# Smaller turns for a recurrence that runs beside attention, with its matrix products a turn later

## The chip, the core and the metric

One NeuronCore of a Trainium2 chip runs the whole kernel. The metric is the device time of one execution in microseconds; lower is better. The five engines have a queue each and take it in order: TensorE (PE in the profile, with its weight loads as PEld), VectorE (DVE), ScalarE (ACT), GpSimd (POOL) and SyncE (SP), which here issues nearly all DMA transfers.

## The reference, cut to what matters

Two layers, each with three token mixers side by side on 1024 latent and 256 context tokens, then an output projection, a gated residual and a squared-ReLU MLP. The mixers are a Fourier group, a bidirectional mLSTM recurrence (4 heads of 96, called the recurrence below) and multi-head latent attention (4 heads):

```
h = modulate(rmsnorm(x, g_norm1[l]), sh1, sc1)
pf, mq, mk, mv, mo, mg, cq, ckv, kr = split_proj(h @ w_in[l])
y_f = fourier_mix(pf)
hf, _ = mlstm_direction(fwd, st_f, False)      # state C_new = decay*C + (wk*k)^T v, chunk by chunk
hb, _ = mlstm_direction(bwd, st_b, True)       # out h = (s@v + w_inter*(q@C)) / max(|den|, exp(-m_t))
y_m = mlstm_output(hf, hb, mo, g_mlstm[l])     # rmsnorm(hf + hb) per head, gated by sigmoid(mo)
y_a = merge_heads(blocked_attend(qn, qr, (lat_keys, ctx_keys)))
x = x + ga1 * (concat([y_f, y_m, y_a]) @ w_out[l])
x = x + ga2 * sqrelu_mlp(modulate(rmsnorm(x, g_norm2[l]), sh2, sc2), w_up[l], w_down[l])
```

## The kernel before, in words

Python code emits instructions, and a scheduler then puts each engine's instructions into a fixed order by priority (the place in the program, unless raised) and by when it expects their inputs; an engine's order on the chip is that order. So where code is written decides the order only in part.

Per layer the kernel runs the input projections, then the attention stage, then the output projection and the MLP. The change touches the attention stage alone. Its main loop goes over blocks (a head, and 512 latent or 256 context queries), and inside over the 10 (context: 2) tiles of 128 keys. One such tile is called a step here, numbered from 0: 88 steps in layer 0, 80 in layer 1. A step computes scores `s` (three products: L138, L143, L144), their exponentials `PT` on ScalarE (L1140), and the value product `v<-PT,Vt` (L1141), which adds to the block's sum. Layer 0 has one PSUM buffer for `s`, layer 1 has two.

TensorE's time between scores and value product is filled with other work. A list `bg` holds the preparation of later blocks: keys and queries (`K`, `Q`, products of `ckn`, `wkv`, `cqn`, `wq`), the maxima of the scores (product L1003 into `m`, maximum `mx` on VectorE L1004, transposed as a row by L1013) and the division at a block's end (`ya`, `rc`, L1031 and L1037). After each step `side_work` pulls turns from a generator: first `mlstm`, then, when that is exhausted, `fourier`. A turn is what the generator emits up to its next `yield`.

`mlstm` has two passes over chunks of 128 tokens. The first (18 steps, two directions `d`) transposes keys (`kt`, L834), weights the values (`wv`, VectorE L839), multiplies them (L842), updates the state `C` on VectorE (L850) and stores it in DRAM (`dC`). It is one turn a step. The second pass takes the chunks in token order. Its first turn is the score product `sp` (L885). Then, for each direction, one turn loads `Mb`, `Wb` and the stored state `Cp`, builds the weights `tm` (L897, ScalarE's exponentials L900, L901) and `qw` (L906), multiplies (`po`, L912 with `tm`, L914 with `qw` and `Cp`) and divides (`dn`, `hd`, L918 to L922). The function `tail` normalises the chunk before and transposes it (L868) for the store of `ym` into `dy`, in one turn. Of these 18 + 4 x 10 = 58 turns of layer 0, 23 are pulled ahead of the main loop, one for each entry of the first `bg` list, at raised priority; the rest goes out at a rate of `nm_ / (tot * RM[l])` turns a step, where `tot` is 78 steps in layer 0 and 70 in layer 1. `RM` thus is the share of the steps over which the recurrence is spread. `fourier` follows at a rate of its own, `nf_ / (tot * RF)`.

The last block (L1119 on) closes the generators' pools, opens the ring of weight buffers in their place, loads `w_out` (`wf`, split by ScalarE and GpSimd into `wr` high and low), loads the mixers' outputs from `dy` (`q`, `qf`, split by ScalarE and VectorE into `A`) and starts the output projection (`mm`, L138, L140, L141) between its steps. In all order listings below, numbers behind names count buffers; `x`, in `s<-Q,x`, is a key tile.

Of the kernel before, what the change touches and what calls it, by code (L numbers as in the profile page):

```python
# [22 lines left out]
C_ID, C_CC, C_SS, C_MK, C_AR, C_RP, C_AC = 0, 128, 256, 384, 640, 1152, 2176  # L23
NCST = 2178
BIG = 1e30
RM = (0.5, 0.8)
GR = (2, 0, 2, 2, 2, 1)
RF = 0.18
LT = (3,)
# [34 lines left out]
def build(tc, A, out, dbg=None):  # L64
# [41 lines left out]
    V, S, G, PE = nc.vector, nc.scalar, nc.gpsimd, nc.tensor  # L106
# [44 lines left out]
    hk = {}  # L151
# [276 lines left out]
    for l in range(2):  # L428
# [384 lines left out]
        def mlstm(mlp_):  # L813
# [12 lines left out]
            for p in range(9):  # L826
                for d in range(2):
                    ci = order[d][p]
                    kc = T(mlp_, [96, 4, 128], tag="kc", bufs=2)
                    nc.sync.dma_start(kc, dkh[:, :, tok(ci)])  # L830
                    vc = load_v(ci)
                    ps = T(psL, [128, 512], tag="l")
                    for h in range(4):
                        PE.transpose(ps[:, h * 96:(h + 1) * 96], kc[:, h, :], ident[:96, :96])  # L834
                    kt = T(mlp_, [128, 512], tag="tm", bufs=2)
                    S.copy(kt[:, :384], ps[:, :384])
                    wcol = wkT[:, 64 * d + ci:64 * d + ci + 31:10]
                    wv = T(mlp_, [128, 4, 128], tag="Mb", bufs=2)
                    V.tensor_tensor(wv[:, :, :97], vc, wcol.unsqueeze(2).to_broadcast([128, 4, 97]), ALU.mult)  # L839
                    pc = T(psL, [128, 512], tag="l")  # L840
                    for h in range(4):
                        PE.matmul(pc[:96, h * 97:(h + 1) * 97], kt[:, h * 96:(h + 1) * 96], wv[:, h, :97], start=True, stop=True)  # L842
                    C = T(mlp_, [96, 4, 128], tag=("qw", "Wb")[d], bufs=2)
                    pv = pc[:96, :388].rearrange("p (h e) -> p h e", h=4)
                    if p == 0:
                        S.copy(C[:, :, :97], pv)
                    else:
                        for h in range(4):
                            dcol = 40 * d + 10 * h + ci
                            V.scalar_tensor_tensor(C[:, h, :97], prev[d][:, h, :97], decb[:, dcol:dcol + 1], pv[:, h], ALU.mult, ALU.add)  # L850
                    prev[d] = C
                    nc.sync.dma_start(dC[d, ci].rearrange("p (h e) -> p h e", h=4), C[:, :, :97])
                    yield
            def tail(ci, hs, mo):
                hsum = hs[0]
                V.tensor_tensor(hsum, hs[0], hs[1], ALU.add)
                S.activation(hs[1], hsum, AF.Square)
                v4 = T(mlp_, [128, 4], tag="v4", bufs=2)
                V.tensor_reduce(v4, hs[1], AX.X, ALU.add)
                V.tensor_scalar(v4, v4, 1.0 / 96, EPS, ALU.mult, ALU.add)  # L860
                y4 = T(mlp_, [128, 4], tag="y4", bufs=2)
                rstd_small(y4, v4, 4, mlp_)
                V.tensor_tensor(hsum, hsum, y4.unsqueeze(2).to_broadcast([128, 4, 96]), ALU.mult)
                hf = hsum.rearrange("p h e -> p (h e)")
                V.scalar_tensor_tensor(mo, mo, 1.0, hf, ALU.add, ALU.mult)
                pt = T(psL, [128, 512], tag="l")
                for i in range(3):
                    PE.transpose(pt[:, i * 128:(i + 1) * 128], mo[:, i * 128:(i + 1) * 128], ident)  # L868
                ym = T(mlp_, [128, 3, 128], tag="ym", bufs=2)
                for i in range(3):  # L870
                    S.activation(ym[:, i], pt[:, i * 128:(i + 1) * 128], AF.Copy, scale=gmh[:, 3 * l + i:3 * l + i + 1])
                nc.sync.dma_start(dy[256:640].rearrange("(i p) t -> p i t", p=128)[:, :, tok(ci)], ym)

            pend = None
            for ci in range(10 if ctx_all else 8):
# [14 lines left out]
                for d in range(2):  # L890
# [12 lines left out]
                    if not first:  # L903
                        pi = order[d][order[d].index(ci) - 1]
                        qw = T(mlp_, [96, 4, 128], tag="qw", bufs=2)
                        V.tensor_tensor(qw, qc, Wb, ALU.mult)  # L906
                        Cp = T(mlp_, [96, 4, 97], tag="Cp", bufs=2)
                        nc.sync.dma_start(Cp, dC[d, pi].rearrange("p (h e) -> p h e", h=4))
                    po = T(psL, [128, 512], tag="l")
                    for h in range(4):  # L910
                        o = po[:, h * 97:(h + 1) * 97]
                        PE.matmul(o, tm[:, h], vc[:, h], start=True, stop=first)  # L912
                        if not first:
                            PE.matmul(o, qw[:, h], Cp[:, h], start=False, stop=True)  # L914
                    pv = po[:, :388].rearrange("p (h e) -> p h e", h=4)
# [7 lines left out]
                    hs.append(hd)  # L923
                    yield
                    if d == 1 and pend is not None:
                        tail(*pend)
                        yield
                pend = (ci, hs, mo)
            tail(*pend)
            yield  # L930


# [138 lines left out]


        mlq = Pools()
        gm_ = mlstm(mlq("ml", side=other))
        bg = [k_rope] + [lambda b=b: k_piece(0, b) for b in (2, 0, 1)] + prepare(0, 0) + [lambda t=t: v_piece(0, t) for t in range(5)]
        p1 = tc.cur_priority - p0
        for f_ in bg:
            with tc.high_priority(offset=p1):
                pull(gm_, 1)
                f_()  # L1080
        fq = None
        steps = [10 if qb < 2 else 2 for _, qb in blocks]
# [19 lines left out]
                        quota["g"] = None  # L1102
                        break

        nm_ = 18 + 4 * (10 if ctx_all else 8) - len(bg) + 1
        nf_ = (7 if ctx_all else 4) * 2 + 1
        quota = dict(m=0.0, f=0.0, g=None, rm=nm_ / (tot * RM[l]), rf=nf_ / (tot * RF))
        ending = None
        for bi, (h, qb) in enumerate(blocks):
# [26 lines left out]
            for i, kt in enumerate(kts):  # L1136
                ps = T(psS, [128, 512], tag="s")
                mm3(ps[:, :nq], K[:, 0, tok(kt)], K[:, 1, tok(kt)], Q[:, 0, :nq], Q[:, 1, :nq], True, True)
                PT = T(atp, [128, 512], tag="PT", bufs=5)
                S.activation(PT[:, :nq], ps[:, :nq], AF.Exp, scale=scale)  # L1140
                PE.matmul(po[:97, :nq], Vt[kt // 2][:, kt % 2, h % 2], PT[:, :nq], start=i == 0, stop=i == len(kts) - 1)  # L1141
                if h == 1 and qb == 1 and kt % 2:
                    v_piece(1, kt // 2)
                while bg and len(bg) > nbg * (len(kts) - 1 - i) / len(kts):
                    bg.pop(0)()
                if not lastb:
                    side_work()
                elif i == 0:
                    while bg:
                        bg.pop(0)()  # L1150
                    wo.append(wtile(A["w_out"][l, 0]))
                    for b in border[:-1]:
                        load_y(b)
                elif i in (1, 3, 5, 7):
                    wo.append(wtile(A["w_out"][l, len(wo)]))
                    if i in LT:
                        out_tile(LT.index(i), 0)
# [544 lines left out]
```

## Time and profile before

| | |
|---|---|
| median of 3 runs | 3015.47 us (3014.15 to 3018.77) |
| the profiled execution's own time | 3019.14 us |
| its span, first to last instruction | 3017.3 us, mean granted TensorE clock 0.962 |
| TensorE busy | 2827.9 us (94%) |
| VectorE busy | 2128.6 us (71%) |
| ScalarE busy | 1178.6 us (39%) |
| attention steps of layer 0 | about 386 to 700 us |
| attention steps of layer 1 | about 1976 to 2250 us |

Times in the profile count from the span's start. A wait in the profile is put down to the engine and the tile that came last. A row of the stretches has start and end, length, busy time of the engines with the number of instructions, the granted clock, and the DMA engines' share and rate. A row of the waits has who waited and for whom, the total in us, the number of waits and the longest. A timeline row has start, duration, engine, line, operation, and in square brackets the idle time ahead of it and what ended it.

### The profile page before, as it was taken

How to read it: one execution, taken by the hardware profiler on the slowest of the kernel's cores; microseconds unless marked ns; L12 is line 12 of the kernel's file. 1: busy time of each engine (PE TensorE's matmuls, PEld its weight loads, DVE VectorE, ACT ScalarE, POOL GpSimd, SP SyncE). 2: the span in 40 equal slices, each digit the busy share in tenths (PEclk: the TensorE clock that was granted, in tenths of full speed). 3: DMA queues.
4: the chain of work that ended last, by engine and by line, in shares of the span. 5: the costliest groups of instructions: out<-in, count | busy, mean ns of one | idle time of the engine just before them, and what ended most of it. 6: DMA issues, size and time to landing. Idle time of an engine off the chain costs nothing.

```text
span 3017.3 us, 40556 instructions
## 1 busy us (share of the span) xinstructions
PE 2827.9 (94%) x14320; PEld 2334.7 (77%) x14320; DVE 2128.6 (71%) x4170; ACT 1178.6 (39%) x2283; POOL 517.3 (17%) x517
## 2 busy tenths in 40 slices
PE   7988989989989999999999898899999999989996
PEld 6877867757878888888887787867767788868885
DVE  8769668742498898786787527468633976678887
ACT  3322245443353333243245432245433534334444
POOL 4213100011200000021125133100022000013334
PEclk7999999999999999999999999899999999999998
DMA  6514575323355544633121212455134443253321
GB/s 237 161 55 128 146 174 156 110 91 120 109 175 175 168 171 165 240 112 116 45 91 56 88 42 85 124 147 147 56 120 139 146 134 115 105 198 99 105 85 56
DMA packets 277871, 376.44 MB, mean 125 GB/s; under 512 B 63396, under 2 KB 154468, under 8 KB 276004
## 3 DMA queue, kind: packets, MB, share of 16 engines
q1 hardware_dynamic: 274788, 366.51, 39.0%
q0 software_dynamic: 576, 4.20, 0.4%
q10 hardware_dynamic: 2304, 3.15, 0.3%
q8 instruction: 113, 1.85, 0.3%
q14 instruction: 90, 0.74, 0.1%
HBM read 283.74 MB, written 90.02 MB: 124 GB/s over the span
## 4 chain that ended last, share of the span: by engine, by line
PE 59%; DVE 18%; DMA 10%; issue 6%; POOL 2%; ACT 2%; SPq 0%; DVEq 0%; POOLq 0%; ACTq 0%
PE mm L138 9%; PE mm L143 7%; PE mm L144 7%; PE v L1141 4%; PE mm L135 4%; PE mm L136 4%; PE mm L134 4%; DVE junk L235 3%; DVE A L148 2%; DVE ac L677 2%; PE mm L1466 2%; PE mm L140 2%; PE mm L141 2%; DMA wf<-in_w_mt 2%; PE t L1466 2%
## 5 line engine op out<-in xcount | busy, mean ns | idle before, releaser
L138 PE MATMUL mm<-A,wr 128*128 128x512 f32 (+1 forms) x840 | 312.9, 375 | 24.6 <-ACT rb L673 12.3
L135 PE MATMUL mm<-A 128*128 128x512 f32 (+1 forms) x654 | 251.3, 389 | 11.2 <-DVE A L148 8.9
L134 PE MATMUL mm<-A 128*128 128x512 f32 (+1 forms) x654 | 238.1, 387 | 5.6 <-ACT A L147 4.4
L136 PE MATMUL mm<-A 128*128 128x512 f32 (+1 forms) x654 | 242.9, 387 | 0.3 <-DVE A L148 0.3
L138 PEld LDWEIGHTS mm<-A,wr 128*128 128x128 f32 x840 | 161.2, 193 | 54.0 <-ACT rb L673 14.0
L143 PE MATMUL mm<-A,wr 128*128 128x512 f32 (+1 forms) x520 | 193.0, 372 | 6.2 <-DVE A L148 4.2
L144 PE MATMUL mm<-A,wr 128*128 128x512 f32 (+1 forms) x520 | 191.6, 369 | 0.0
L1141 PE MATMUL v<-PT,Vt 128*97 128x512 f32 (+1 forms) x336 | 172.8, 599 | 16.6 <-ACT PT L1140 16.1
L138 PE MATMUL mm<-A,c 128*128 128x512 f32 (+1 forms) x520 | 184.0, 355 | 4.5 <-ACT A L147 3.4
L143 PE MATMUL mm<-A,c 128*128 128x512 f32 (+1 forms) x520 | 184.3, 355 | 2.7 <-DVE A L148 2.6
L144 PE MATMUL mm<-A,c 128*128 128x512 f32 (+1 forms) x520 | 182.5, 353 | 1.3 <-DVE c L148 1.3
L148 POOL TENSOR_TENSOR wr<-wf,wr 128x512 fp32r<-128x512 f32 x88 | 123.7, 1413 | 292.1 <-ACT wr L147 230.3
L147 ACT ACTIVATE A<-wr 128x512 fp32r<-128x512 f32 x188 | 114.2, 625 | 147.9 <-PE mm L135 59.2
L147 ACT ACTIVATE A<-A 128x512 fp32r<-128x512 f32 x174 | 106.9, 625 | 160.0 <-PE mm L135 86.6
L148 DVE TENSOR_TENSOR A<-wr,A 128x512 fp32r<-128x512 f32 x146 | 128.7, 893 | 43.4 <-ACT A L147 29.0
L235 DVE SCALAR_TENSOR_TENSOR junk<-wf,t 128x512 bf16<-128x512 f32 x192 | 130.8, 681 | 33.7 <-DMA wf<-in_w_mt 32.0
L135 PEld LDWEIGHTS mm<-A 128*128 128x128 f32 x654 | 123.9, 190 | 39.4 <-DVE A L148 11.7
L1140 ACT ACTIVATE PT<-s 128x512 f32<-128x512 f32 (+1 forms) x168 | 97.0, 583 | 138.6 <-PE s L144 138.0
L134 PEld LDWEIGHTS mm<-A 128*128 128x128 f32 x654 | 123.1, 189 | 31.2 <-ACT A L147 6.8
L136 PEld LDWEIGHTS mm<-A 128*128 128x128 f32 x654 | 123.5, 189 | 25.0 <-DVE A L148 0.7
L138 PE MATMUL mm<-wr,A 128*128 128x256 f32 x464 | 133.4, 288 | 6.6 <-ACT rb L673 4.7
L143 PE MATMUL mm<-wr,A 128*128 128x256 f32 x464 | 133.1, 288 | 0.0
(497 smaller groups left out, 7802.9 us busy)
## 6 DMA issues: line engine op xcount, KB each, us to landing
wf<-in_w_mt SPq DMA_DIRECT2D x96, 256.0 KB
x<-in_w_up SPq DMA_DIRECT2D x40, 512.0 KB
r<-in_w_up SPq DMA_DIRECT2D x38, 512.0 KB
wr<-in_w_dn SPq DMA_DIRECT2D x36, 512.0 KB
gt<-in_w_mt SPq DMA_DIRECT2D x64, 256.0 KB
da<-wf SPq DMA_DIRECT2D x64, 256.0 KB
da<-p SPq DMA_DIRECT2D x64, 256.0 KB
wf<-in_w_in SPq DMA_DIRECT2D x56, 256.0 KB
```

What stands on the lines that cost most here:

```text
L134: PE.matmul(ps, lh, rh, start=first, stop=False, skip_group_check=True)
L135: PE.matmul(ps, lh, rl, start=False, stop=False, skip_group_check=True)
L136: PE.matmul(ps, ll, rh, start=False, stop=last, skip_group_check=True)
L138: PE.matmul(ps, lh, rh, start=first, stop=False)
L143: PE.matmul(ps, lh, rl, start=False, stop=False)
L144: PE.matmul(ps, ll, rh, start=False, stop=last)
L147: (hi or S).activation(dst[0], src, AF.Copy) if (hi is None or hi is S) else hi.tensor_copy(dst[0], src)
L148: (lo or G).tensor_tensor(dst[1], src, f32(dst[0]), ALU.subtract)
L235: V.scalar_tensor_tensor(junk, f, 1.0, cb[w], ALU.mult, ALU.mult, accum_out=(ga, modT[l])[kh][:, w, j:j + 1])
L1140: S.activation(PT[:, :nq], ps[:, :nq], AF.Exp, scale=scale)
L1141: PE.matmul(po[:97, :nq], Vt[kt // 2][:, kt % 2, h % 2], PT[:, :nq], start=i == 0, stop=i == len(kts) - 1)
L1466: PE.matmul(o, blk[f"B{h + 1}{q + 1}"][k][:, 128 * jj:128 * jj + 128], f[:, k, 256 * h:256 * h + 256], start=h + k == 0, stop=h * k == 3)
```

## The change

It splits the recurrence's turns. In the first pass a `yield` stands between the weighting on VectorE and the products on TensorE; in the second, between the elementwise preparation and the `po` products; in `tail`, between the normalisation and the transposes. The turns are 36 + 7 x 10 = 106 in layer 0; two instead of one are pulled for each entry ahead of the loop (46 for 23), and the count `nm_` follows. The `po` products with `tm` and the transposes in `tail` get an edge behind the latest value product: on TensorE they may not be ordered ahead of the value product that was the last one emitted. `RM` of layer 0 goes from 0.5 to 0.75; that of layer 1 stays 0.8.

```diff
-RM = (0.5, 0.8)
+RM = (0.75, 0.8)
...
                     V.tensor_tensor(wv[:, :, :97], vc, wcol.unsqueeze(2).to_broadcast([128, 4, 97]), ALU.mult)
+                    yield
                     pc = T(psL, [128, 512], tag="l")
...
+            def after_pv():
+                return behind("pv" if hk.get("pv") else None)
+
             def tail(ci, hs, mo):
...
                 V.scalar_tensor_tensor(mo, mo, 1.0, hf, ALU.add, ALU.mult)
+                yield
                 pt = T(psL, [128, 512], tag="l")
                 for i in range(3):
-                    PE.transpose(pt[:, i * 128:(i + 1) * 128], mo[:, i * 128:(i + 1) * 128], ident)
+                    with after_pv():
+                        PE.transpose(pt[:, i * 128:(i + 1) * 128], mo[:, i * 128:(i + 1) * 128], ident)
...
                         nc.sync.dma_start(Cp, dC[d, pi].rearrange("p (h e) -> p h e", h=4))
+                    yield
                     po = T(psL, [128, 512], tag="l")
                     for h in range(4):
                         o = po[:, h * 97:(h + 1) * 97]
-                        PE.matmul(o, tm[:, h], vc[:, h], start=True, stop=first)
+                        with after_pv():
+                            PE.matmul(o, tm[:, h], vc[:, h], start=True, stop=first)
...
                     if d == 1 and pend is not None:
-                        tail(*pend)
+                        yield from tail(*pend)
                         yield
...
+        hk["pv"] = None
         gm_ = mlstm(mlq("ml", side=other))
...
-                pull(gm_, 1)
+                pull(gm_, 2)
...
-        nm_ = 18 + 4 * (10 if ctx_all else 8) - len(bg) + 1
+        nm_ = 36 + 7 * (10 if ctx_all else 8) - 2 * len(bg) + 1
...
-                PE.matmul(po[:97, :nq], Vt[kt // 2][:, kt % 2, h % 2], PT[:, :nq], start=i == 0, stop=i == len(kts) - 1)
+                hk["pv"] = PE.matmul(po[:97, :nq], Vt[kt // 2][:, kt % 2, h % 2], PT[:, :nq], start=i == 0, stop=i == len(kts) - 1)
```

What it does to the order, at three places of layer 0. First TensorE at the second pass's first chunk, steps 14 and 15 before (L912 and L914 are its products; `l_4085` is the forward direction, `l_4123` the backward one):

```order
L912 MATMUL l_4085<-vc_4050,tm_4074 128x97
L914 MATMUL l_4085<-Cp_4083,qw_4081 128x97
L1141 MATMUL v_4688<-PT_4759,Vt_589_3482 97x512
L914 MATMUL l_4123<-Cp_4121,qw_4119 128x97
L912 MATMUL l_4123<-vc_4050,tm_4112 128x97
L914 MATMUL l_4123<-Cp_4121,qw_4119 128x97
L912 MATMUL l_4123<-vc_4050,tm_4112 128x97
L914 MATMUL l_4123<-Cp_4121,qw_4119 128x97
```

The same chunk now, steps 13 and 14 (L920 and L922 are L912 and L914, L1150 is L1141):

```order
L922 MATMUL l_4085<-Cp_4075,qw_4073 128x97
L920 MATMUL l_4085<-vc_4050,tm_4066 128x97
L920 MATMUL l_4123<-vc_4050,tm_4104 128x97
L922 MATMUL l_4085<-Cp_4075,qw_4073 128x97
L920 MATMUL l_4085<-vc_4050,tm_4066 128x97
L922 MATMUL l_4085<-Cp_4075,qw_4073 128x97
L1150 MATMUL v_4612<-PT_4649,Vt_588_3481 97x512
L138 MATMUL s_4679<-Q_4316,x_586_3479 128x512
L922 MATMUL l_4123<-Cp_4113,qw_4111 128x97
```

Both directions still come close together, a step earlier than before; the backward one now has a score product ahead of its products with `Cp`.

Second, TensorE at the end of the sixth block of 512, steps 63 to 65 before:

```order
L1141 MATMUL v_6356<-PT_6479,Vt_591_3484 97x512
L138 MATMUL s_6488<-Q_6099,x_586_3479 128x512
L143 MATMUL s_6488<-Q_6099,x_586_3479 128x512
L144 MATMUL s_6488<-Q_6099,x_586_3479 128x512
L1141 MATMUL v_6356<-PT_6492,Vt_592_3485 97x512
L138 MATMUL s_6501<-Q_6099,x_586_3479 128x512
L143 MATMUL s_6501<-Q_6099,x_586_3479 128x512
L144 MATMUL s_6501<-Q_6099,x_586_3479 128x512
L1141 MATMUL v_6356<-PT_6505,Vt_592_3485 97x512
```

The last of these steps now (`l<-tb,uc` and `l<-tb,uh` are Fourier products):

```order
L138 MATMUL s_6357<-Q_5805,x_586_3479 128x512
L143 MATMUL s_6357<-Q_5805,x_586_3479 128x512
L144 MATMUL s_6357<-Q_5805,x_586_3479 128x512
L138 MATMUL l_6373<-tb_6184,uc_6344 128x128
L143 MATMUL l_6373<-tb_6184,uc_6344 128x128
L144 MATMUL l_6373<-tb_6184,uc_6344 128x128
L786 MATMUL l_6373<-tb_6184,uh_6352 128x128
L787 MATMUL l_6373<-tb_6184,uh_6352 128x128
L138 MATMUL l_6379<-tb_6184,uc_6349 128x128
L143 MATMUL l_6379<-tb_6184,uc_6349 128x128
L144 MATMUL l_6379<-tb_6184,uc_6349 128x128
L1150 MATMUL v_6070<-PT_6361,Vt_592_3485 97x512
```

Steps that held nothing between scores and value product hold Fourier products.

Third, SP where the weights of the output projection are first loaded, before:

```order
L811 DMA dy_91<-yt_6091 128x1280 [waits DMAHW0_49,DVE_49,Activation_49]
L1039 DMA dy_91<-ya_6517 96x512 [waits DMAHW1_49,DVE_49]
L167 DMA wf_6760<-in_w_out 128x512 [waits DMAHW2_49,PE_49]
L167 DMA wf_6765<-in_w_out 128x512 [waits DMAHW3_49]
L167 DMA wf_6843<-in_w_out 128x512 [waits DMAHW4_49]
L1057 DMA q_1492_6771<-dy_91 128x512 [waits DMAHW5_49,DVE_49]
```

And now (L1065 is L1057, a load of the mixers' outputs; `yt` is the second and last Fourier output):

```order
L1065 DMA q_1492_6771<-dy_91 128x512 [waits DMAHW1_49,DVE_49]
L1065 DMA qf_6775<-dy_91 128x512 [waits DMAHW2_49,DVE_49]
L1065 DMA q_1494_6779<-dy_91 128x512 [waits DMAHW3_49,DMAHW1_49,DVE_49]
L1065 DMA qf_6783<-dy_91 128x512 [waits DMAHW4_49,DMAHW2_49,DVE_49]
L811 DMA dy_91<-yt_6420 128x1280 [waits DMAHW5_49,DVE_49,Activation_49]
L1065 DMA q_1496_6787<-dy_91 128x512 [waits DMAHW6_49,DMAHW3_49,DVE_49]
L167 DMA wf_6760<-in_w_out 128x512 [waits DMAHW7_49,PE_49]
L167 DMA wf_6765<-in_w_out 128x512 [waits DMAHW0_49]
L167 DMA wf_6843<-in_w_out 128x512
```

The weights' first loads have moved behind the last Fourier store and five loads of the mixers' outputs. The first product that needs them stands in step 76 of TensorE's order instead of step 72.

More of the change, by code (lines that the diff above doesn't have):

```diff
@@ L925, in mlstm @@
                     if d == 1 and pend is not None:
-                        tail(*pend)
+                        yield from tail(*pend)
                         yield
                 pend = (ci, hs, mo)
-            tail(*pend)
+            yield from tail(*pend)
             yield
```

## The prediction

> **What bounds the kernel now.** I read the page's first part, then the stretches of the two attention stages, then who waited for whom in each stretch, then the timeline at the places found.
>
> ```profile
> span 3017.3 us, 40556 instructions
> PE 2827.9 (94%) x14320; PEld 2334.7 (77%) x14320; DVE 2128.6 (71%) x4170; ACT 1178.6 (39%) x2283; POOL 517.3 (17%) x517
> ```
>
> TensorE is the bound, and the change adds and removes no matrix product. So it can only move TensorE's gaps, and what follows from gaps. The stages that it touches are these (TensorE, weight loads, VectorE, ScalarE, GpSimd busy; then granted clock and DMA):
>
> ```profile
> 427.00:456.00 29.00, 23.99 (x120) 17.41 (x119) 21.23 (x46) 11.68 (x29) 0.11 (x1) 0.88 0.58 158
> 456.00:576.00 120.00, 114.07 (x666) 86.11 (x666) 106.08 (x339) 64.40 (x165) 1.27 (x8) 1.00 0.55 154
> 576.00:629.00 53.00, 52.64 (x285) 38.89 (x284) 32.57 (x73) 21.81 (x56) 0.23 (x3) 1.00 0.10 35
> 656.00:692.00 36.00, 29.54 (x112) 20.75 (x111) 11.55 (x23) 14.34 (x27) 7.69 (x6) 0.81 0.45 135
> 1976.00:2140.00 164.00, 155.73 (x866) 119.11 (x866) 127.14 (x354) 77.11 (x179) 1.26 (x12) 0.96 0.50 126
> 2140.00:2215.00 75.00, 74.99 (x344) 52.69 (x343) 42.70 (x86) 35.09 (x70) 12.59 (x10) 0.98 0.35 113
> 443.60:450.40 6.80, 6.40 (x19) 4.32 (x18) 4.21 (x10) 2.13 (x7) 0.00 (x0) 0.50 0.63 147
> 668.90:682.60 13.70, 10.14 (x33) 7.44 (x31) 2.79 (x7) 3.23 (x8) 0.00 (x0) 0.50 0.30 90
> 2044.50:2051.30 6.80, 6.80 (x28) 5.88 (x27) 5.96 (x21) 2.57 (x6) 0.00 (x0) 0.50 0.41 105
> 2123.00:2129.80 6.80, 6.80 (x27) 6.20 (x27) 3.71 (x10) 1.80 (x4) 0.00 (x0) 0.50 0.19 56
> ```
>
> While the recurrence's second pass runs (427 to 576) VectorE is busy 127.3 of 149 us and TensorE idles 10.9 us, and 8.3 us in the same part of layer 1 (1976 to 2140); while the Fourier group fills the steps (576 to 629) TensorE idles 0.4 us; at the end of layer 0 it idles 6.5 of 36 us. Four stretches ran at clock 0.50. The waits behind the gaps, first in 427 to 656, then 656 to 692, then 1976 to 2215, then 2215 to 2270:
>
> ```profile
> PE v L1141 <- ACT PT L1140: 6.2, 10, 1.1
> PE m L1003 <- ACT Q L147: 3.2, 3, 1.6
> PE l L914 <- DMA Cp<-dC: 1.2, 1, 1.2
> PE m L1037 <- DVE rc L1033: 1.1, 1, 1.1
> PE l L912 <- issue: 0.9, 2, 0.7
> PE l L914 <- DVE qw L906: 0.8, 1, 0.8
> ...
> PE v L1141 <- ACT PT L1140: 6.2, 3, 3.5
> ...
> PE m L1013 <- DVE m L1010: 2.6, 2, 1.9
> PE l L914 <- DMA Cp<-dC: 1.8, 1, 1.8
> PE m L1003 <- DVE mx L1004: 1.5, 2, 1.0
> ...
> PE mm L138 <- ACT A L147: 2.5, 1, 2.5
> ```
>
> The largest is not the recurrence's: the value product `v` waits for its exponentials `PT`. Layer 0 has one buffer for scores, so a step with nothing between its scores and its value product stands still:
>
> ```profile
> 630.23 0.40 PE L144 MATMUL s<-Q,x 97*128 97x512 f32 x1
> 631.38 1.10 PE L1141 MATMUL v<-PT,Vt 128*97 128x512 f32 x2 [0.75 <-ACT PT L1140]
> ...
> 633.93 1.10 PE L1141 MATMUL v<-PT,Vt 128*97 128x512 f32 x2 [0.74 <-ACT PT L1140]
> ...
> 635.33 0.39 PE L144 MATMUL s<-Q,KT 97*128 97x512 f32 x1
> 635.71 1.05 PE L1031 MATMUL m<-ones,ya 1*128 1x1 f32 x8
> ```
>
> An empty step takes 2.55 us, 0.75 of them standing; with eight tiny products in between there is no wait.
>
> **The change, part by part.** *The smaller turns* (the new `yield`s) and the new counts issue the same instructions. Turns left for the steps of layer 0: 36 over 39 before (0.92 a step), 61 over 58.5 now (1.04 a step, of smaller turns). The order has the last transposes of the recurrence in step 58 instead of 48, and the Fourier products in steps 58 to 73 instead of 48 to 63. In layer 1, where the share stays 0.8, both still move eight steps later. "Elementwise work on VectorE" moves nothing: those operations were VectorE's before.
>
> *Filler for empty steps, 427 to 656.* I counted in the new order the steps with fewer than four small products between scores and value product, at 0.75 us empty, 0.45 with one or two products, 0.25 with four tiny ones: 6.3 us. Before it is 6.2. What Fourier now fills late (steps 64 and 65 were empty) is lost in the middle, because products ordered behind the value product come ahead of the next scores and leave the place after them empty (steps 42 and 48). Taken: 0, bounds 2 either way.
>
> *Recurrence products a turn later.* Their waits in layer 0 are 1.2 + 0.9 + 0.8 = 2.9 us. A turn is about a step, some 3 us, longer than any of these waits; but the worst, the first two chunks, are as close together in the new order as before. Taken: -2.0, bounds 0 and -2.9. `Q` (3.2) and `rc` (1.1) wait for ScalarE and VectorE behind recurrence work; 0, bounds 3 either way. Layer 1: Cp 1.8, taken -1.5; the maxima (2.6 + 1.5) wait for VectorE, whose load there is the same: 0, bounds -4 and +2.
>
> *The new edge to the value product* is order on TensorE alone, no semaphore. Behind a late product wait only its own VectorE readers, the store of `ym` and the two-buffer tiles (`Cp`, `qw`, `tm`, `hd`), whose next loads on SP come later by the same turn; nothing is recurrent in this pass, since the states are already in `dC`. No cost taken.
>
> *End of layer 0.* Here lies the largest term. ScalarE takes its queue in order, and the exponentials stood behind splits that waited for loads:
>
> ```profile
> 645.77 1.28 SPq L167 DMA_DIRECT2D wf<-in_w_out  x3
> 648.53 0.33 SPq L1057 DMA_DIRECT2D q<-dy  x1
> 651.40 0.33 SPq L1057 DMA_DIRECT2D qf<-dy  x1
> ...
> 649.53 4.24 POOL L148 TENSOR_TENSOR wr<-wf,wr 128x512 fp32r<-128x512 f32 x3 [50.00 <-DMA wf<-in_w_out]
> 666.25 0.63 ACT L147 ACTIVATE wr<-wf 128x512 fp32r<-128x512 f32 x1 [2.18 <-DMA wf<-in_w_out]
> 666.79 0.58 ACT L1140 ACTIVATE PT<-s 128x512 f32<-128x512 f32 x1
> 671.92 0.42 ACT L147 ACTIVATE A<-q 128x256 fp32r<-128x256 f32 x1 [3.08 <-DMA q<-dy]
> 672.25 0.58 ACT L1140 ACTIVATE PT<-s 128x512 f32<-128x512 f32 x1
> ```
>
> That cost most of 6.2 us, and the half-speed stretch behind it 10.14 / 2 = 5.1 us. In the new order five loads of `y` go ahead of the weights on SP, the first output-projection products come in step 76 instead of 72, and every step from 76 to 83 holds some. So these two waits should go, up to -10.5 with the clock. Against it stands the weights' later start: they queue behind the last Fourier store. From issue to the end of the first low half it took 3.8 us plus a third of 4.24, 5.2 us. Between the last Fourier product and the first that needs weights lie two nearly empty steps of 2.55 us and the first 1.4 us of a third (633.93 to 635.33), 6.5 us; the store's own work before it takes 1 to 2 us. So cover and need are about equal; I keep 4 of the 10.5 for new waits. Taken: -6.5, bounds -10.5 and the slower rival below.
>
> *Half-speed stretches in the middle.* The first stands where gaps crowd (427 to 445):
>
> ```profile
> 445.02 2.02 PE L1141 MATMUL v<-PT,Vt 128*97 128x512 f32 x2 [0.40 <-ACT PT L1140]
> 450.95 1.02 PE L1141 MATMUL v<-PT,Vt 128*97 128x512 f32 x2
> ```
>
> It costs 6.40 / 2 = 3.2 us, the two in layer 1 3.4 each. If fewer gaps crowd, some go: taken -2.0 of 10.0, bounds 0 and -10. [...]
>
> *End of layer 1.* 2.5 us for `A`; Fourier and weights also move late there. Taken 0, bounds -2.5 and +4.
>
> **Sum.** -2.0 - 1.5 - 6.5 - 2.0 = -12.0 us. The profiled execution took 3019.14 us (span 3017.3), 3.7 above the median of 3015.47; the gaps are no longer for that, so I take the difference over: 3015.5 - 12.0 = 3003.5.
>
> **Rivals.** *The clock does not follow short waits:* then the middle's 2.0 falls away, and the end's 5.1 stays in the sum, since a wait of 3.5 us stood there: 3005.5. For it: 2123 falls to half speed with no wait above 0.7 us on its list (2.6 less 1.9), so something else may set the clock. Against it: 443.6. [...] *Gaps only move:* the filler count (6.3 against 6.2) says so for layer 0's middle; if new waits of the same kind stand at the end too, 3015. *All goes:* the end term whole, half of the middle stretches' 10.0, the products' waits whole: -10.5 - 5 - 2.9 - 1.8 = -20.2, and with some of `Q` and the maxima below 2995; the two late stretches at 0.4 and 0.0 us idle show that a filled step can be gapless. *Slower, one mechanism:* SP takes its queue in order too, and ahead of the last Fourier store stand four `y` loads on two buffers; before, such loads came 2.9 us apart (648.53, 651.40). If those are held up as then, the weights start up to 12 us late (four times 2.9). It decides once the weights' issue is over 1.5 us behind the last Fourier store. Price: 12 us of wait, 5 us of half speed, and no gain at the end: 3003.5 + 6.5 + 17 = 3027. Against it: the loads' inputs are long in memory, and their splits stand early on ScalarE.
>
> **How the numbers follow.** Under 0.2% (6.0 us) a measurement of this kernel can't tell from no change. Forecast (2995 to 3009.4) 0.38; clock rival 0.12; all goes 0.13; gaps move 0.23; slower 0.14. So faster 0.63, same 0.23, slower 0.14. The range runs from 2988 to 3022: it leaves out about half of "all goes" and most of the slower case. The forecast alone: 2995 to 3009.
>
> **What would show it.** The last recurrence transposes about ten steps later and Fourier filling to the end: busy near 53 of 53 us there. No wait of `v` over 1 us and no half-speed stretch where the weights arrive; if that stretch is there, the largest term is wrong. Waits of `l` for Cp or qw under 1 us in sum. Wrong altogether if `wf` is issued many us after the last Fourier product, or if `m` or `Q` waits grow as VectorE's turns stand ahead of the maxima.

## The result, and the profile after

Beside each other, the kernel before took 3017.1 us (median of 4 runs) and the changed kernel 2999.4 (4 runs): ratio 0.9949, 95% interval 0.9932 to 0.9967, some 15 us less. In a second comparison (the last experiment below) the ratio was 0.9962, interval 0.9948 to 0.9976, some 11.5 us less. Two executions far from all others, 4813 us of the kernel before and the profiled 10459 us of one experiment's kernel, are in no ratio. The forecast was 12.0 us less. The sum came out right; the parts under it did not all, as the stages show.

The profile's first part, of the changed kernel:

```profile
span 2996.5 us, 40533 instructions
PE 2816.8 (94%) x14320; PEld 2328.0 (78%) x14320; DVE 2131.9 (71%) x4170; ACT 1179.5 (39%) x2283; POOL 509.0 (17%) x517
```

TensorE's gaps are the span less its busy time: 189.4 us before, 179.7 now. To see where, I cut the attention stages at the same steps in both traces. The rows are steps 0 to 12, 12 to 40, 40 to 54 and 54 to 87 of layer 0, then steps 88 to 128 and 128 to 167 of layer 1 and the 50 to 56 us behind its last value product (columns as in the prediction: length, TensorE, weight loads, VectorE, ScalarE, GpSimd, clock, DMA share). Before:

```profile
387.90:425.80 37.90, 37.51 (x257) 29.54 (x255) 28.81 (x84) 15.36 (x30) 1.15 (x11) 1.00 0.80 173
425.80:547.50 121.70, 111.68 (x629) 83.66 (x628) 103.46 (x301) 61.37 (x157) 0.84 (x8) 0.97 0.61 164
547.50:596.60 49.10, 48.08 (x270) 35.31 (x270) 37.23 (x111) 23.82 (x61) 0.67 (x3) 1.00 0.27 85
596.60:722.40 125.80, 113.80 (x486) 79.02 (x485) 46.72 (x97) 47.35 (x96) 18.48 (x15) 0.95 0.28 90
1980.00:2133.60 153.60, 145.33 (x810) 111.28 (x809) 121.22 (x337) 73.39 (x172) 1.15 (x11) 0.96 0.51 131
2133.60:2247.40 113.80, 112.44 (x495) 77.45 (x494) 55.83 (x116) 47.31 (x91) 15.16 (x12) 0.99 0.32 102
2247.40:2300.00 52.60, 50.06 (x219) 40.56 (x218) 12.89 (x19) 14.36 (x23) 16.59 (x13) 0.97 0.41 134
```

And of the changed kernel:

```profile
384.10:424.30 40.20, 36.73 (x244) 28.66 (x242) 29.00 (x85) 16.42 (x34) 1.04 (x10) 0.97 0.72 171
424.30:536.40 112.10, 107.78 (x613) 81.66 (x613) 100.74 (x289) 58.91 (x147) 0.73 (x7) 0.98 0.63 165
536.40:583.30 46.90, 43.05 (x225) 29.93 (x223) 32.24 (x91) 20.65 (x47) 0.64 (x2) 1.00 0.12 35
583.30:707.80 124.50, 118.08 (x547) 84.29 (x546) 56.25 (x122) 51.46 (x114) 18.08 (x17) 0.99 0.37 117
1959.00:2102.90 143.90, 138.26 (x761) 104.06 (x760) 113.44 (x313) 69.84 (x162) 1.16 (x11) 0.96 0.55 136
2102.90:2224.00 121.10, 119.84 (x559) 84.41 (x558) 63.35 (x139) 52.00 (x103) 15.53 (x13) 1.00 0.33 104
2224.00:2280.00 56.00, 50.33 (x219) 40.94 (x218) 12.22 (x18) 14.48 (x23) 16.95 (x14) 0.94 0.40 131
```

Length less TensorE's busy time is the idle time. Half speed costs half of TensorE's busy time inside the half-speed stretches, as in the prediction (the pair of value products shown there took 2.02 us at 445.02, at a granted clock of 0.50, and 1.02 at 450.95, behind the stretch); idle time there is counted already, and the rows' clock is rounded, so I add up the stretches themselves. The work in a row is not quite the same in both kernels (turns moved), so I compare these two, not the lengths.

| steps | idle before | now | cost of half speed before | now |
|---|---|---|---|---|
| 0-12 | 0.4 | 3.5 | 0 | 0.5 |
| 12-40 | 10.0 | 4.3 | 3.2 | 2.3 |
| 40-54 | 1.0 | 3.9 | 0 | 0 |
| 54-87 | 12.0 | 6.4 | 5.0 | 1.7 |
| layer 1, 88-167 | 9.6 | 6.9 | 8.5 | 5.1 |
| behind it | 2.5 | 5.7 | 1.7 | 1.9 |

(Sums in the text are taken before rounding.) Layer 0 gains 5.4 us of idle time and 3.8 of half speed; layer 1 gains 6.1 in its steps and loses 3.3 behind the last one. The waits in layer 0, steps 12 to 64 and then 64 to 87, and behind layer 1's last step:

```profile
PE v L1150 <- ACT PT L1149: 3.6, 7, 0.7
PE l L920 <- DVE tm L907: 1.1, 1, 1.1
PE m L1011 <- ACT Q L147: 0.7, 1, 0.7
...
PE v L1150 <- ACT PT L1149: 4.7, 8, 0.7
PE m L1039 <- ACT ya L1034: 1.5, 2, 1.0
...
PE mm L138 <- ACT A L147: 5.7, 1, 5.7
```

The two waits of 1.89 and 3.53 us are gone; none of `v` is over 0.7 us. The recurrence's waits for `Cp` and `qw` are gone, one of 1.1 for `tm` came. A new one stands in step 12, where the table has lost 3.1 us. TensorE, then VectorE, then ScalarE there:

```profile
423.38 1.01 PE L1039 MATMUL m<-ones,ya 1*128 1x1 f32 x4 [3.47 <-ACT ya L1034]
...
420.59 0.69 DVE L903 TENSOR_TENSOR tm<-msk,Mb 128x512 f32<-128x512 f32 x1 [5.03 <-DMA Mb<-dM]
...
421.31 1.28 ACT L906 ACTIVATE tm<-tm,aT 128x128 f32<-128x128 f32 x4 [4.60 <-DVE tm L903]
...
422.96 0.36 ACT L1034 COPY ya<-v 97x256 f32<-97x256 f32 x1
```

The chain reads from below: the copy of `ya` (a block's result, for which TensorE's tiny products wait) stands on ScalarE behind `tm`'s exponentials, those behind VectorE's product, and that behind a load of `Mb`. The second pass of the recurrence now reaches its first elementwise turn ahead of that copy; before it came just behind. The load was as late before (6.1 us from its issue at 420.82 to its use at 426.93; now 6.5, from 414.06 to 420.59), but then the copy did not stand behind it:

```profile
426.93 0.69 DVE L897 TENSOR_TENSOR tm<-msk,Mb 128x512 f32<-128x512 f32 x1 [4.14 <-DMA Mb<-dM]
...
422.47 0.37 ACT L1026 COPY ya<-v 97x256 f32<-97x256 f32 x1 [0.77 <-PE v L1141]
```

### The profile page after: what moved, and what is told of

It is laid out like the page before. It is cut to its first block, busy times and chain, and to the rows that moved or that the text cites. A ratio compares the mean times of both kernels' runs of the same rounds, so it can differ in the third digit from the quotient of the medians.

```text
span 2996.5 us, 40533 instructions
## 1 busy us (share of the span) xinstructions
PE 2816.8 (94%) x14320; PEld 2328.0 (78%) x14320; DVE 2131.9 (71%) x4170; ACT 1179.5 (39%) x2283; POOL 509.0 (17%) x517
## 4 chain that ended last, share of the span: by engine, by line
PE 60%; DVE 17%; DMA 9%; issue 6%; POOL 3%; ACT 2%; SPq 0%; DVEq 0%; POOLq 0%; ACTq 0%
PE mm L138 9%; PE mm L143 7%; PE mm L144 7%; PE v L1150 4%; PE mm L135 4%; PE mm L136 4%; PE mm L134 3%; DVE junk L235 3%; DMA wf<-in_w_mt 2%; DVE ac L677 2%; PE mm L140 2%; PE mm L141 2%; PE mm L1475 2%; DVE A L148 2%; PE t L1475 2%
## 5 line engine op out<-in xcount | busy, mean ns | idle before, releaser
L135 PE MATMUL mm<-A 128*128 128x512 f32 (+1 forms) x654 | 251.2, 389 | 12.3 <-DVE A L148 10.0
L1150 PE MATMUL v<-PT,Vt 128*97 128x512 f32 (+1 forms) x336 | 172.7, 596 | 9.7 <-ACT PT L1149 8.8
L138 PE MATMUL mm<-wr,A 128*128 128x256 f32 x464 | 134.0, 289 | 7.6 <-ACT rb L673 4.6
L148 DVE TENSOR_TENSOR A<-A,A 128x512 fp32r<-128x512 f32 x131 | 115.5, 890 | 27.1 <-ACT A L147 25.1
```

What stands on the lines that cost most here:

```text
L135: PE.matmul(ps, lh, rl, start=False, stop=False, skip_group_check=True)
L138: PE.matmul(ps, lh, rh, start=first, stop=False)
L148: (lo or G).tensor_tensor(dst[1], src, f32(dst[0]), ALU.subtract)
L1150: hk["pv"] = PE.matmul(po[:97, :nq], Vt[kt // 2][:, kt % 2, h % 2], PT[:, :nq], start=i == 0, stop=i == len(kts) - 1)
```

## The experiments

Ratios are against the kernel before, run beside each, with 95% intervals; about 3015 us times one less the ratio is the gain. They were run in three groups, each on a chip of its own: the first four below; then both with loads ahead, the splits and the second pass alone; then both with the own buffer, the first pass alone and the changed kernel again. So in the first two groups the changed kernel itself is missing, and its ratios from outside stand for it. Where two intervals overlap, I do not tell the kernels apart.

**The spread alone.** On the kernel before:

```
-RM = (0.5, 0.8)
+RM = (0.75, 0.8)
```

> The kernel before with the share of layer 0 raised from 0.5 to 0.75 and nothing else. In its order the recurrence ends in step 50 and Fourier in step 67, but the five y loads do not move ahead of the output weights. My theory (the gain is made of removed gaps, the largest part being the new order at the end of layer 0): the value product's waits of 1.9 and 3.5 us and the 13.7 us half-speed stretch at the end of layer 0 stay, so the time is within 4 us of before. Rival A (the later spread itself gains, by filling the empty steps 64 and 65): 8 to 12 us faster than before, wherever the loads stand.

Ratio 0.9997 (0.9987 to 1.0008): nothing. At the end of layer 0 the row of steps 54 to 87 and its first wait:

```profile
588.90:717.80 128.90, 118.65 (x523) 83.83 (x522) 50.84 (x102) 48.76 (x102) 19.00 (x17) 0.96 0.29 90
...
PE v L1141 <- ACT PT L1140: 8.0, 5, 5.2
```

The empty steps 64 and 65 hold Fourier products, yet 10.3 us are idle (12.0 before), 5.2 of them in one wait of `v` at the weights.

**The changed kernel with the old spread.** The same line the other way, on the changed kernel.

> The changed kernel with the share of layer 0 back at 0.5. From step 53 to the end of layer 0 its order is that of before. My theory: the two long waits and the half-speed stretch at the end of layer 0 are back (6 to 10 us of the gain lost), the smaller turns keep some 3 to 7 us in the middle of layer 0 and in layer 1: 3 to 8 us faster than before. Rival A (the spread gains): no different from before. Rival B (smaller turns and the edge do it all, the end does not matter): as fast as the changed kernel, 13 us or more faster than before.

Ratio 0.9986 (0.9973 to 0.9998), 4 us, as my theory had it. The end is as before, a wait of 3.9 us in 9.1 and clock 0.96:

```profile
591.20:716.80 125.60, 113.29 (x485) 78.68 (x484) 46.93 (x97) 47.35 (x96) 18.50 (x15) 0.96 0.29 90
...
PE v L1150 <- ACT PT L1149: 9.1, 8, 3.9
```

**Without the edge.**

```
 def after_pv():
-    return behind("pv" if hk.get("pv") else None)
+    return behind(None)
```

> The changed kernel without the edge to the latest value product; turns and shares as changed. Its order has the recurrence end in step 52 instead of 57, Fourier in 68 instead of 72, and the loads of y behind the first output weights as before; layer 1 ends Fourier in step 147 as before. My theory: the end of layer 0 is slow as before (waits of value products of 1.5 us and more, a half-speed stretch of 10 us or more), the turns keep part of the middle: 3 to 8 us faster than before. Rival B (the edge orders only TensorE and costs or brings nothing by itself): as fast as the changed kernel, 13 us or more faster than before.

Ratio 0.9964 (0.9950 to 0.9978), 11 us: more than my theory gave, and the interval overlaps both of the changed kernel's. What the edge brings is too little to tell. Its end, in which the loads stand in nearly the old order:

```profile
585.10:709.20 124.10, 115.97 (x525) 82.59 (x524) 51.47 (x105) 49.03 (x105) 18.55 (x17) 0.97 0.31 97
...
PE v L1150 <- ACT PT L1149: 3.6, 4, 1.5
PE m L1039 <- ACT ya L1034: 2.4, 1, 2.4
```

8.1 us idle, between 12.0 before and 6.4. Fourier ends in step 68 here and in 67 with the spread alone, which idles 10.3; what differs besides is that three of the first five loads of `y` stand one weight earlier. The waits are of the same kind (ScalarE held by splits that wait for loads), only shorter. That the loads must all go ahead of the weights, as I had it, is not so.

**Layer 1's share at 0.65.** `RM = (0.75, 0.65)` on the changed kernel.

> The changed kernel with the share of layer 1 lowered from 0.8 to 0.65, which moves its last recurrence products from step 144 to 134 and Fourier's end from 155 to 147, where they stood before. Layer 0 is as changed. My theory: the wait of 5.7 us for A at the end of layer 1 shrinks to some 2.5 us, as before, while recurrence turns stand somewhat closer: within 4 us of the changed kernel, 11 to 19 us faster than before. Rival C (layer 1's gain in the middle came from its turns standing later): 6 us or more slower than the changed kernel, with the half-speed stretches at steps 108 to 128 back.

Ratio 0.9949 (0.9936 to 0.9962): as the changed kernel. The wait for `A` behind layer 1 was 3.0 us (5.7), the idle time of steps 88 to 167 went from 6.9 to 8.3. Rival C's loss isn't there: that layer 1's turns stand later neither gains nor costs anything that can be told.

**Loads one turn ahead.** On the changed kernel, the second pass issues its loads a turn earlier:

```
 S.copy(ssb, sp)
+mw = [load_mw(0), None]
 yield
...
-    Mb, Wb loaded here
+    Mb, Wb = mw[d]
...
+    if d == 0:
+        mw[1] = load_mw(1)
     yield
```

> The changed kernel, with the loads of Mb and Wb for each half of a chunk issued one turn ahead of the elementwise work that reads them; turns and shares unchanged. Theory on the new wait (3.5 us in step 12: the copy of ya stands on ScalarE behind exponentials of tm, these behind VectorE's product for tm, and that behind a load of Mb that takes 6 us from its issue): the wait falls below 1 us, the 1.9 us wait of s for Q in layer 1 as well, and the time falls 3 to 8 us against the changed kernel, so 18 to 26 us faster than before. Rival: the load is late because of the queue of transfers, not of where it is issued; the wait stays at 3 us and the time as the changed kernel's, 13 to 17 us faster than before.

Ratio 0.9968 (0.9954 to 0.9981), no faster than the changed kernel: my theory failed. The wait was still 3.0 us. In the order built from it SP has the first loads of `Mb` where they were, since they wait for their buffer, which products of the first pass hold. SP's and VectorE's lines:

```profile
416.97 0.54 SPq L900 DMA_DIRECT2D Mb<-dM  x1
...
423.02 0.69 DVE L909 TENSOR_TENSOR tm<-msk,Mb 128x512 f32<-128x512 f32 x1 [4.55 <-DMA Mb<-dM]
```

It took 6.05 us from issue to use (6.5 in the changed kernel), so up to here the rival fits as well: the wait stayed, and the load may be slow wherever it is issued.

**A buffer of its own.** So the first pass got another buffer for direction 1:

```
-wv = T(mlp_, [128, 4, 128], tag="Mb", bufs=2)
+wv = T(mlp_, [128, 4, 128], tag="Mb", bufs=2) if d == 0 else T(mlp_, [128, 512], tag="ssb").rearrange("p (h e) -> p h e", h=4)
```

> The changed kernel with one line changed: in the recurrence's first pass the weighted values of direction 1 take the buffer of ssb, which is free there, instead of one of the two buffers that Mb uses in the second pass. In its order the first load of Mb stands five places earlier on SP and both copies of ya in step 12 stand ahead of tm's exponentials. Theory (moving the load a turn ahead in the program did nothing because the load waits for its buffer): the wait for ya in step 12 falls from 3.0 to 3.5 us to under 1 us, the wait of s for Q in layer 1 from 1.9 to under 1 us; 2 to 7 us faster than the changed kernel run beside it. Rival (the load of Mb is late because of the transfers ahead of it): tm still waits 2 us or more for Mb and some other wait takes the place; the same as the changed kernel.

Ratio 0.9993 (0.9984 to 1.0001): nearly all of the gain lost. The order did what was meant, and the wait for `ya` is gone, but others stand in steps 0 to 12:

```profile
386.70:434.60 47.90, 41.92 (x257) 32.06 (x255) 30.53 (x89) 16.87 (x36) 1.05 (x10) 0.93 0.68 154
...
PE l L834 <- DVE qw L851: 3.2, 3, 1.6
PE l L834 <- DVE tm L903: 2.7, 1, 2.7
...
419.28 0.38 SPq L901 DMA_DIRECT2D Mb<-dM  x1
...
426.31 0.69 DVE L903 TENSOR_TENSOR tm<-msk,Mb 128x512 f32<-128x512 f32 x1 [0.85 <-DMA Mb<-dM]
```

The first pass's transposes now wait for VectorE, 5.9 us in four waits, and the load of `Mb` was in use 7.0 us behind its issue. The theory had the wait for `ya` right and the time wrong; the rival had it right that other waits take the place, but `tm` waits 0.85 us for `Mb`, not 2, and the time is worse than it said. Neither way brought a gain; the loads several turns ahead, or the copy of `ya` put ahead by an edge, were not tried.

**Loads ahead, layer 1's share at 0.65**, both edits above, on the changed kernel:

> The kernel with the loads of Mb and Wb one turn ahead, and layer 1's share at 0.65 instead of 0.8 (its recurrence ends in step 134 instead of 144, Fourier in 147 instead of 155). Expected from the two alone: the wait for A at the end of layer 1 3.0 us instead of 5.7, step 12 and Q as in the run with the loads alone: 18 to 28 us faster than before, the fastest of all. Rival: closer turns in layer 1 bring back waits there (2 us or more for Cp, tm or the maxima), and it is no faster than the one with the loads alone.

Ratio 0.9947 (0.9926 to 0.9968), 16 us, short of the 18 expected, and not told apart from the changed kernel's. **Own buffer and the share at 0.65:**

> As the run with the own buffer, and layer 1's share at 0.65 instead of 0.8. Expected: step 12 and Q as there, the wait for A at the end of layer 1 about 3 us instead of 5.7; 4 to 10 us faster than the changed kernel run beside it, and 18 to 25 us faster than before. Rival: what is saved at the end of layer 1 comes back as waits among the closer turns; no faster than the own buffer alone.

Ratio 0.9971 (0.9961 to 0.9981), 9 us; the changed kernel beside it 0.9962. No gain over it, so the expectation failed; but it is faster than the own buffer alone (0.9993), so the rival failed too. No profile of this kernel is read, so where that comes from is open.

**The splits off ScalarE.** On the kernel before, the last block of layer 0:

```
-split((r[:, 0], r[:, 1]), f, lo=...)
+split((r[:, 0], r[:, 1]), f, hi=V if l == 0 else None, lo=...)
...
-split((yT[b][:, 0, k], yT[b][:, 1, k]), yf[:, :n], lo=V)
+split((yT[b][:, 0, k], yT[b][:, 1, k]), yf[:, :n], hi=V if l == 0 and b != border[-1] else None, lo=V)
```

> The kernel before, with the upper halves of the splits of the output weights and of y in the last block of layer 0 computed on VectorE instead of ScalarE. Turns, shares and the order of the loads there are those of before; in layer 1 the order shifts by a few steps. My theory on the end of layer 0 (exponentials stand on ScalarE behind splits that wait for loads): the value product's waits of 1.9 and 3.5 us fall below 1 us each and the half-speed stretch of 13.7 us shrinks to 6.8 or less, so the part from step 54 to 87 takes 5 to 9 us less than before's 125.8; the whole 4 to 10 us faster than before. Rival (the steps are empty and TensorE would wait for the weights themselves in any case): the waits move to the output products, that part takes the same 125 us, and the whole is within 2 us of before.

Ratio 0.9988 (0.9973 to 1.0003), not told apart from before, where I expected 4 us or more. The end of layer 0:

```profile
591.70:714.90 123.20, 113.25 (x485) 78.03 (x484) 59.85 (x123) 33.83 (x70) 19.75 (x15) 0.97 0.29 92
...
PE v L1141 <- ACT PT L1140: 4.1, 6, 0.7
PE mm L138 <- DVE A L147: 1.6, 1, 1.6
PE m L1037 <- DVE rc L1033: 1.4, 2, 1.1
```

With the order of the loads untouched, the long waits of `v` are gone: they did stand behind ScalarE's splits. But the part takes 2.6 us less and not 5 to 9; 3.0 us came back as waits of the output products and of `rc` for VectorE. Both the theory and its rival hold in part.

**The second pass's turns alone** (the first pass's new `yield` taken out of the changed kernel, its counts as before):

> The changed kernel without the new turn in the recurrence's first pass (18 turns there, one pulled with each piece, as before); the second pass, the edge and the shares as changed. In its order the copy of ya in step 12 stands ahead of tm's exponentials again. My theory (the middle's gain is the second pass's): steps 12 to 40 idle at most 5 us, as in the changed kernel, against 9.9 before; the 3.5 us wait for ya is gone: 0 to 6 us faster than the changed kernel, 15 to 21 us faster than before. Rival (the first pass's turn carries part of the gain): steps 12 to 40 idle 7 us or more, and the time is 4 us or more behind the changed kernel's.

Ratio 0.9975 (0.9962 to 0.9989), 7.5 us. My theory failed, as the rows below show. **The first pass's turn alone** (on the kernel before):

> The kernel before with the new turn in the recurrence's first pass and nothing else: second pass in its old turns, no edge, shares 0.5 and 0.8. Theory after the run with the second pass alone (steps 12 to 40 idled 10.0 us there, so that part of the gain is the first pass's): steps 12 to 40 idle 5 us or less against 9.9 before, a wait of about 3.5 us for ya in step 12, the end of layer 0 as before (two waits of v, a half-speed stretch of 10 us or more); 2 to 6 us faster than before. Rival (the two passes' turns gain only together): steps 12 to 40 idle 8 us or more; within 2 us of before.

Ratio 0.9998 (0.9986 to 1.0010). Steps 12 to 40 of the two, first the second pass alone with two of its waits, then the first pass alone:

```profile
421.20:540.80 119.60, 109.62 (x611) 81.90 (x612) 100.90 (x291) 59.56 (x152) 0.73 (x7) 0.97 0.60 159
...
PE m L1010 <- ACT Q L147: 1.8, 1, 1.8
...
PE m L1044 <- DVE rc L1040: 1.2, 1, 1.2
```

```profile
429.10:547.40 118.30, 113.06 (x640) 86.84 (x640) 101.67 (x297) 60.88 (x155) 0.85 (x8) 0.95 0.62 161
```

With the second pass alone these steps idle 10.0 us, as before; with the first pass alone 5.2, near the changed kernel's 4.3 (in its one profile half speed cost 5.3 us there, against 3.2 before). So it is the edit of the first pass, which the prediction hardly looked at, that took most of the 5.7 us out of there, and it also brought the new wait. That edit is two things: the `yield`, and two turns pulled ahead of the loop for each entry. By the counts 10 turns of the second pass go out ahead of the loop with it (46 less the first pass's 36), and 5 without (23 less 18). Which of the two clears steps 12 to 40, no run shows. In steps 0 to 12 of the first pass alone stands:

```profile
PE m L1032 <- ACT ya L1027: 4.3, 1, 4.3
```

With the second pass alone these steps idle 0.4 us. By itself the first pass's turn gains nothing.

**The changed kernel again**, beside these:

> The changed kernel itself, beside the others, to compare with them on one chip and to see what a second profile of the same program shows. Expected: 12 to 18 us faster than before; idle time of the two attention stages within 2 us of the first profile's 18.8 and 6.9; the stages that no edit touches up to 6 us different from the first profile, because half-speed stretches fall elsewhere. Rival (the gain seen first was partly luck): less than 10 us faster than before.

Ratio 0.9962 (0.9948 to 0.9976): 11.5 us, just under what I expected and above the rival's 10, which the interval (7 to 16 us) does not exclude. Its profile:

```profile
span 3012.7 us, 40533 instructions
PE 2833.2 (94%) x14320; PEld 2339.2 (78%) x14320; DVE 2133.1 (71%) x4170; ACT 1179.4 (39%) x2283; POOL 512.9 (17%) x517
```

The same program is 16.2 us longer here, and idle for 179.5 us instead of 179.7. All of the difference is busy time, that is, clock: 236 us at half speed against 206 in the first profile (229 before). One pair of profiles can't carry a difference of 12 us. The idle time of the attention stages can be compared: in each row of the table it is within 0.6 us of the first profile's.

## Why the prediction was right, and where its steps were not

*End of layer 0, taken -6.5, bound -10.5.* Right in kind, too small. The two waits went, and of the half-speed stretch of 13.7 us 3.4 are left (at 667.7, shown below); idle time fell 5.6 us and the cost of half speed 3.3 in steps 54 to 87, together 8.9. Of the 4 us that I kept for new waits 1.6 appeared. The slower rival's point was 1.5 us between the last Fourier store and the weights; it was 1.15:

```profile
647.15 0.32 SPq L811 DMA_DIRECT2D dy<-yt  x1
...
648.30 1.76 SPq L167 DMA_DIRECT2D wf<-in_w_out  x3
```

The cause was half right: the run with the splits on VectorE shows that exponentials waited behind them; the run without the edge shows that most of the end's idle time goes without all five loads moved.

*Filler, taken 0.* Held: without the two long waits, `v` waits for `PT` 9.2 us in steps 12 to 87 before and 8.3 now. As the prediction had it, the middle pays: steps 40 to 54 idle 2.8 us more.

*Products' waits, taken -2.0 and -1.5.* `Cp` and `qw` went in both layers as said, but others took their place: 1.1 us for `tm` and 0.6 for issue in layer 0, where 1.2 of the 2.9 us were gained, and 1.7 for issue in layer 1, where next to nothing of the 1.8 was. *The maxima, taken 0:* in layer 1 they fell from 4.1 to 1.8 us, inside the bounds, but a wait of 1.9 us of `s` for `Q` came. *`Q` and `rc`, taken 0, bounds 3:* `Q` fell from 3.2 to 0.7, `rc` from 1.1 to 0.3 (now for `rs_t`), together 3.3 us. This step failed in its reason: I held these waits to come from VectorE's and ScalarE's load, which is unchanged; they went with the edit of the first pass (the run without it still waits 1.8 and 1.2 us for them, the run with it alone for neither).

*No cost for the new edge.* No run shows one. The cost that I missed is the turn's: I named who waits behind a late *product*, not who stands on ScalarE behind a late *elementwise* turn. That is `ya`, 3.5 us and a half-speed stretch that began 1.4 us before that wait ended, at 422.0 (2.7 us, half of 5.42). Three half-speed stretches of the changed kernel, at `ya`, at the weights of layer 0 and behind layer 1's last step:

```profile
422.00:428.80 6.80, 5.42 (x16) 4.04 (x17) 3.44 (x7) 3.70 (x11) 0.00 (x0) 0.50 0.90 203
667.70:671.10 3.40, 3.40 (x7) 2.00 (x7) 1.36 (x3) 1.75 (x4) 1.86 (x2) 0.51 0.82 246
2237.90:2244.70 6.80, 3.72 (x9) 2.95 (x10) 2.98 (x5) 3.15 (x5) 0.00 (x0) 0.50 0.87 258
```

*Half speed in the middle, taken -2.0 of 10.* Too small for one profile and too large for the other: steps 12 to 54 and 88 to 167 lost 11.7 us to it before, 7.4 in the first profile after, and 11.0 in the second.

*End of layer 1, taken 0, bounds -2.5 and +4.* Inside, near the bad end: the wait for `A` grew from 2.5 to 5.7 us (5.4 in the second profile) and the half-speed stretch at it from 3.4 to 6.8 us, nearly half of that idle; together 3.3 us lost. From layer 1's first value product to the end of the program it took 1037.3 us before, 1037.5 and 1041.3 after: layer 1 gained nothing that can be told, where the sum had -1.5 for `Cp` and a part of the -2.0.

Added up over the table's rows, the first profile gives 12.1 us less and the second, counted in the same way, 7.0; most of what lies between them, 3.4 us, is half speed in layer 1. That the first equals the forecast is luck in its parts: the end of layer 0 gave 2.4 us more than taken and steps 12 to 40 gave 6.7 where the sum had at most 4.0, while steps 0 to 12 (3.5), steps 40 to 54 (2.8) and the end of layer 1 (3.3), each taken as 0, took that back. The rest of the measured 11.5 to 15 us lies in stages that the change hardly touches, and one profile of each doesn't tell it from chance: the first 385 us alone idled 43.4 to 50.1 us over 13 profiles, and the 50.1 is the kernel before's.

What carries the gain is the combination: spread alone 0, first pass alone 0, all turns with the old spread 4, second pass with the spread 7.5, all of it without the edge 11, all of it 11 to 15 (neighbours in this list are not told apart, its ends are). The stages fit: steps 54 to 87 idle 12.3 us with the old spread and 10.3 with the spread alone, but 5.2 with the spread and the second pass's turns; steps 12 to 40 idle 10.0 there and 4.0 with all turns and the old spread. The whole has both. "Gaps only move", a rival with 0.23, describes the spread and the first pass alone, and not the whole.

## What to carry to other kernels

When a piece of work is moved or cut, go through each in-order queue that it issues on and ask what stands behind it there if its input is late; here a load that took 6.5 us from issue to use held VectorE (5.0 us), ScalarE (4.6) and then TensorE (3.5) in a step that had no gap before. Parts of a change can each be worth nothing and together something, so undo them one at a time *and* try them alone. Compare idle time stage by stage, and not spans, between two single profiles where the clock moves.

## What the runs showed of the hardware

The half-speed stretches lie on a grid: in the traces' clock records each lasts a multiple of 3.41 us (3.4 to 13.7 us, and 30.7 us for the first one: 29 of 30 stretches in the kernel before, 24 of 25 in the changed kernel's first profile), but for the last one, of 26.0 and 23.3 us, which goes on past the last instruction. I laid TensorE's idle time of 13 profiles on that grid and looked at stretches at full clock. With 2.0 us or more idle in a cell of 3.41 us the next cell was at half speed in 238 of 238 cases; with 1.5 to 2.0 in 81 of 136; with 0.75 to 1.5 in 41 of 346; below that in 20 of 9834. The kernel before and the changed kernel's first profile alone have 32 of 32, 13 of 25, 7 of 64 and 3 of 1512. (Where the count begins moves these by a few cells.) The prediction's four stretches, at 443.6, 668.9, 2044.5 and 2123, had 1.6, 1.9, 2.8 and 1.1 us idle in the cell ahead. One case of the changed kernel's second profile, the cell ahead and the stretch:

```profile
424.60:428.00 3.40, 0.35 (x2) 0.00 (x0) 1.80 (x6) 1.07 (x4) 0.00 (x0) 1.00 0.60 146
428.00:434.80 6.80, 5.81 (x17) 4.22 (x18) 3.35 (x7) 3.31 (x9) 0.00 (x0) 0.50 0.77 198
```

The idle time of a cell need not be one gap: the 2.8 us ahead of the stretch at 2044.5 in the kernel before are two waits, of 0.96 and 1.89 us. Counted from a program's first instruction the grid lies differently in each profile (its first line at 3.3 us in the kernel before, 2.1 and 1.4 in the changed kernel's two), so the same two gaps can fall into one cell in one execution and into two cells in the next. That fits the 16.2 us between two profiles of one program with equal idle time, but no run shows it to be their cause. The first rival, in which the clock follows no short wait, falls: the waits right ahead of the stretches at 443.6, 668.9 and 2044.5 were of 1.6, 1.9 and 1.9 us, and the counts above go with the idle time. The wait of 3.5 us for which that rival kept the end's 5.1 stood inside the stretch at 668.9, from 669.35 to 672.88.
